# Hybrid decoder layer: key rotations and the first conv blob in the written-order stage, compression later, eight gate columns beside w_out

## Chip, cores and metric

One core of a Trainium2 chip runs the whole layer in one launch. The metric is the device time in microseconds, the median of three runs. TensorE multiplies (PE, with PEld for its weight loads), VectorE is DVE, ScalarE is ACT, GpSimd is POOL, and SP issues most DMAs.

## The reference, cut to what matters

```python
mod_all = silu(c) @ W_ada + b_ada            # 6 x 2048: sh1, sc1, g1, sh2, sc2, g2
h = rms_norm(x, g1n) * (1 + sc1) + sh1       # 512 tokens x 2048
u = h @ w_in                                 # u_b, u_c, u_h, q, kc, vc, ksl, vsl, kwn, vwn, gates
y_conv = u_b * (conv_b + sum_k conv_w[k] * shift(u_c * u_h, 2 - k))
k_cmp = compress(rope(kc)); v_cmp = compress(vc)     # gelu(blocks @ w1) @ w2
y_attn = nsa_attention(rope(q), k_cmp, v_cmp, rope(ksl), vsl, rope(kwn), vwn, sigmoid(gates))
x = x + g1 * (concat(rms_norm(y_conv), rms_norm(y_attn)) @ w_out)
h = rms_norm(x, g2n) * (1 + sc2) + sh2
x = x + g2 * (relu(h @ w_ff1) ** 2 @ w_ff2)
out = rms_norm(x)
```

All arrays are float32. There are 8 query heads and 2 key-value heads of 128, and the feed-forward width is 8192.

## The kernel before

Activations lie transposed: features on the 128 partitions, 512 tokens along the row. Every float32 product is done in three float32r matmuls (`mm3`, L92): high by high, high by low, low by high. So each weight blob of 128 x 1024 (512 KB) that arrives in `raw` is split by `weights` (L76): ACT copies it to `wh` (L83), VectorE subtracts to get `wl` (L84). `raw` has three buffers, `wh` and `wl` two each. A blob is 24 matmuls of 512 columns.

The modulation `mod` is a matrix-vector product that runs on VectorE, not on TensorE: each of its 96 columns is two blobs of `w_ada`, each multiplied with `cs` (the broadcast SiLU of `c`) and summed in one instruction (`dot`, L131), and then a bias (`bias_in`, L137). 32 columns (shift and scale 1) are needed for the first tokens `hs`. The other 64 stand in `todo` (L248): gate 1, scale and shift 2, gate 2. The last is used only in the feed-forward part.

Instructions are ordered by a list scheduler that works before the run, from its own estimates. Where `pinned` is true, `pin` (L67) keeps the written order on each engine instead. Nearly everything up to L361 is pinned: this is the written-order stage. It runs the 32 `steps` of L284 (16 blobs of `w_kv`, 16 of `w_cv`, in four groups), each with eight output tiles in the eight PSUM banks. At a group's end the eight banks are copied into `part` (first half of the depth) or added to it (L346, second half). Group 0 is `w_kv` (keys and values), group 1 the first eight tiles of the conv projection. Step 23 ends group 0, step 31 ends group 1. `clock` and `ready` are the written plan: `ready` grows by 5.6 a step, and the generator `work` (L265) hands out VectorE work with its estimated costs until `clock` comes within 1.0 of `ready`. That work is the columns of `mod` and the tokens; its blobs come into `ring`, eight `wa` buffers (`ada_steps`, L152).

After the stage (unpinned, L363 on), the keys are rotated: `rope` (L367) is four VectorE instructions, `rope_split` (L374) adds an ACT copy and a VectorE subtraction. `kc` takes two `rope`, `kslc` and `kwin` four `rope_split`. Then the loop over `j` (L485) makes the conv output `y` from three tiles each; the tiles after the eighth come from `project` (L400), two halves of one `w_conv` blob each, 32 halves in all. After each half, `tick` advances the first generator in `background` (the two `compress`, L417) and `more_ada(1)` does one further column of `todo`. A compression first adds position vectors (`ct`), splits them (`chi`, `clo`), then takes eight blobs of `cmp_w1` (`swh`, `swl`). The value and gate projections and the queries follow, each with `more_ada(1)` per blob, then attention with the conv half of `w_out`.

The pool `mainp` has 29 slots of 128 x 1032 float32 that nearly all of these tiles share, `cs`, `wa`, `h_m`, `part`, `y` among them; a tile holds its slot until its last reader.

The other half of `w_out` begins at L783: eight loops over `k`, each with one blob from `raw_blob` (L753, six `rw` buffers), split by `hilo` (L762) into one of three `hl` tiles, and 24 matmuls. Eight `w_oa2` blobs are then split and kept, and the feed-forward part follows.

Of the kernel before, what the change touches and what calls it, by code (L numbers as in the profile page):

```python
# [15 lines left out]
P = 128  # L16
# [24 lines left out]
def hybrid_layer(ctx: ExitStack, tc: tile.TileContext, a, out):  # L41
# [84 lines left out]
    pin(nc.vector.tensor_tensor(out=sc, in0=sc, in1=vec[:, V_C:V_ID], op=OP.mult))  # L126
    pin(nc.scalar.activation(small.tile([P, 1], F32, name="junk"), eps, AF.Sqrt))
    ring = [slot(name="wa")[:, :1024] for _ in range(NWA)]
    turn = [0]
# [10 lines left out]

    def ada(n, early=False):
        acc = small.tile([P, 2], F32, name="acc")
        for i in range(2):
            if early:
                w = slot(name="wa")[:, :1024]
                nc.sync.dma_start(out=w, in_=a["w_ada"][2 * n + i])
            else:
                w = load(a["w_ada"][2 * n + i])[:, :1024]
            dot(w, i, acc)
        bias_in(n, acc)  # L150

    def ada_steps(n):  # L152

        acc = small.tile([P, 2], F32, name="acc")
        for i in range(2):
            w = ring[turn[0] % NWA]
            turn[0] += 1
            pin(nc.sync.dma_start(out=w, in_=a["w_ada"][2 * n + i]))
            dot(w, i, acc)
            if i:  # L160
                bias_in(n, acc)
            yield 1.25
# [78 lines left out]
    for i in range(4):  # L241
# [6 lines left out]
    todo = [M_G1 * NK + k for k in range(NK)] + [w * NK + k for k in range(NK) for w in (M_SC2, M_SH2)] \  # L248
        + [M_G2 * NK + k for k in range(NK)]
    done = [0]  # L250
    rb = accum("rb")
# [9 lines left out]
    def low(h, t):  # L261
        pin(nc.vector.tensor_tensor(out=h[:, 1], in0=t, in1=h[:, 0].bitcast(F32), op=OP.subtract))
        hs.append(h)

    def work():  # L265
# [18 lines left out]
    steps = [("w_kv", k) for k in range(4)] + [("w_cv", k) for k in range(8)] \  # L284
        + [("w_kv", k) for k in range(4, NK)] + [("w_cv", k) for k in range(8, NK)]

    def blob(s):
        return weights(a[steps[s][0]][steps[s][1]])
# [25 lines left out]
    banks = {}  # L314
    for s, (name, k) in enumerate(steps):
        grp = 0 if name == "w_kv" else 1
# [21 lines left out]
        if last:  # L338
            for n in range(8):
# [5 lines left out]
                else:  # L345
                    pin(nc.vector.tensor_tensor(out=part[grp, n], in0=ps[n], in1=part[grp, n], op=OP.add))  # L346
                    clock += 0.7
        while clock < ready - 1.0:
            cost = next(flow, None)
            if cost is None:  # L350
                break
            clock += cost
# [4 lines left out]
        if s == 18:  # L357
            pin(nc.scalar.activation(mask_r, cst[:, :C_CMASK - C_MASK], AF.Copy))
    while turn[0] % 2:
        next(flow)  # L360
    pinned[0] = False  # L361

    def more_ada(n, early=True):  # L363
        for _ in range(min(n, len(todo))):
            ada(todo.pop(0), early)

    def rope(dst, ps):  # L367
        t = pair(name="rt")
        nc.vector.tensor_tensor(out=t[:, 0], in0=ps, in1=cos, op=OP.mult)
        nc.vector.tensor_tensor(out=t[0:64, 1], in0=ps[64:128], in1=sin[64:128], op=OP.mult)  # L370
        nc.vector.tensor_tensor(out=t[64:128, 1], in0=ps[0:64], in1=sin[0:64], op=OP.mult)
        nc.vector.tensor_tensor(out=dst, in0=t[:, 0], in1=t[:, 1], op=OP.add)

    def rope_split(dst, ps, scale):  # L374
        t = temp(name="rs2")
        rope(t, ps)
        nc.scalar.activation(dst[:, 0], t, AF.Copy, scale=scale)
        nc.vector.scalar_tensor_tensor(out=dst[:, 1], in0=t, scalar=scale, in1=dst[:, 0].bitcast(F32),
                                       op0=OP.mult, op1=OP.subtract)

    kc = pair(name="kc")
    vc = [part[0, 2], part[0, 3]]
    for g in range(NG):
        rope(kc[:, g], part[0, g])
    kwin = [pair(F32R, name="kwin") for _ in range(NG)]
    kslc = [attc.tile([P, 2, 32 + T], F32R, name=f"kslc{g}") for g in range(NG)]
    for g in range(NG):
        rope_split(kslc[g][:, :, 32:], part[0, 4 + g], 1.0)
        rope_split(kwin[g], part[0, 6 + g], 1.0)

    background = []

    def tick():
# [23 lines left out]
    def compress(which, src):  # L417
# [3 lines left out]
        for hf in range(2):  # L421
# [14 lines left out]
            nc.vector.tensor_tensor(out=lo, in0=t, in1=hi.bitcast(F32), op=OP.subtract)  # L436
            parts.append((hi, lo))
        pc = bank()
        for blk in range(8):
# [39 lines left out]

    background += [compress(0, [kc[:, 0], kc[:, 1]]), compress(1, vc)]  # L480

# [66 lines left out]
    def head(n):  # L548
        q = pair(F32R, name="q")
        rope_split(q, raws[n], SCALE)  # L550
        qs.append(q)
# [645 lines left out]
```

## Time and profile before

| | |
|---|---|
| median of 3 runs | 2250.53 us (2250.18 to 2252.56) |
| profiled execution | 2251.69 us, span 2249.9 us, mean granted clock 0.974 |
| TensorE busy | 2138.4 us, 95% of the span |
| VectorE busy | 1919.1 us, 85% |
| ACT busy | 1009.5 us, 45% |
| HBM traffic | 383.00 MB read, 68.16 MB written |
| dots of `w_ada` | 192 of 1220 ns: 96 from `ring`, 96 after the stage |
| dots in the last eight steps (183.9 to 229.6 us) | 24 |

A matmul's row gives its start and its modelled length; matmuls overlap, so the distance from start to start is the pace. "[11.58 <-DVE wl L84]" means that the engine had been idle for 11.58 us and that VectorE's `wl` at line 84 ended it. Engine shares are means over the whole span; a change in one stage is read from the busy time of that stage and the waits in it.

### The profile page before, as it was taken

How to read it: one execution, taken by the hardware profiler on the slowest of the kernel's cores; microseconds unless marked ns; L12 is line 12 of the kernel's file. 1: busy time of each engine (PE TensorE's matmuls, PEld its weight loads, DVE VectorE, ACT ScalarE, POOL GpSimd, SP SyncE). 2: the span in 40 equal slices, each digit the busy share in tenths (PEclk: the TensorE clock that was granted, in tenths of full speed). 3: DMA queues.
4: the chain of work that ended last, by engine and by line, in shares of the span. 5: the costliest groups of instructions: out<-in, count | busy, mean ns of one | idle time of the engine just before them, and what ended most of it. 6: DMA issues, size and time to landing. Idle time of an engine off the chain costs nothing.

```text
span 2249.9 us, 37644 instructions
## 1 busy us (share of the span) xinstructions
PE 2138.4 (95%) x14942; PEld 1976.7 (88%) x14942; DVE 1919.1 (85%) x2998; ACT 1009.5 (45%) x1468; POOL 193.5 (9%) x366
## 2 busy tenths in 40 slices
PE   6999699999999999899999999999899999999996
PEld 4777478788877769799999999999899999999996
DVE  8889988776586755999999999999899999999995
ACT  4431233222354433766665666656433333333353
POOL 0000000000000000021111111113211011001100
PEclk8999799999999999899999999999999999999998
DMA  8988378756211134176666666668865466366432
GB/s 345 337 319 312 135 287 349 286 210 247 91 50 57 57 113 167 68 223 200 201 206 202 201 195 197 196 207 256 325 244 186 161 234 235 124 224 243 168 114 94
DMA packets 143984, 453.62 MB, mean 202 GB/s; under 512 B 15808, under 2 KB 20160, under 8 KB 143808
## 3 DMA queue, kind: packets, MB, share of 16 engines
q1 hardware_dynamic: 92192, 323.27, 40.2%
q0 software_dynamic: 51616, 127.95, 17.1%
q8 instruction: 117, 1.92, 0.3%
q14 instruction: 59, 0.48, 0.1%
HBM read 383.00 MB, written 68.16 MB: 201 GB/s over the span
## 4 chain that ended last, share of the span: by engine, by line
PE 78%; DVE 13%; ACT 4%; DMA 3%; issue 2%; SPq 0%; DVEq 0%; ACTq 0%
PE pf L93 19%; PE pf L95 19%; PE pf L94 19%; PE ps L95 5%; PE ps L94 5%; PE ps L93 5%; DVE scr L133 3%; DVE wl L84 2%; DMA wa<-in_w_ada 1%; PE pw L94 1%; PE pw L95 1%; PE pw L93 1%; DVE hl L764 1%; PE pt L683 1%; ACT wh L83 1%
## 5 line engine op out<-in xcount | busy, mean ns | idle before, releaser
L95 PE MATMUL pf<-tk,hl 128*128 128x256 f32 x3576 | 1007.1, 282 | 13.0 <-DVE hl L764 13.0
L93 PE MATMUL pf<-tk,hl 128*128 128x256 f32 x3576 | 1009.7, 283 | 9.6 <-ACT hl L763 8.2
L94 PE MATMUL pf<-tk,hl 128*128 128x256 f32 x3576 | 1007.1, 282 | 1.2 <-DVE tk L834 1.2
L95 PEld LDWEIGHTS pf<-tk,hl 128*128 128x128 f32 x3576 | 677.9, 190 | 15.6 <-DVE hl L764 15.5
L93 PEld LDWEIGHTS pf<-tk,hl 128*128 128x128 f32 x3576 | 679.2, 190 | 12.2 <-ACT hl L763 10.9
L94 PEld LDWEIGHTS pf<-tk,hl 128*128 128x128 f32 x3576 | 678.1, 190 | 1.6 <-DVE tk L834 1.5
L763 ACT ACTIVATE hl<-rw 128x1024 fp32r<-128x1024 f32 x266 | 280.8, 1057 | 291.6 <-PE pf L95 266.8
L764 DVE TENSOR_TENSOR hl<-rw,hl 128x1024 fp32r<-128x1024 f32 x266 | 324.5, 1221 | 48.4 <-ACT hl L763 48.0
L763 ACT ACTIVATE hl<-sg 128x1024 fp32r<-128x1024 f32 x189 | 200.4, 1061 | 268.6 <-PE pf L95 241.7
L764 DVE TENSOR_TENSOR hl<-sg,hl 128x1024 fp32r<-128x1024 f32 x189 | 230.8, 1222 | 42.2 <-ACT hl L763 42.1
L133 DVE SCALAR_TENSOR_TENSOR scr<-wa,cs 128x1024 bf16<-128x1024 f32 x192 | 229.7, 1220 | 6.2 <-DMA wa<-in_w_ada 6.1
L83 ACT ACTIVATE wh<-raw 128x1024 fp32r<-128x1024 f32 (+1 forms) x103 | 108.8, 1060 | 238.9 <-PE ps L94 137.9
L84 DVE TENSOR_TENSOR wl<-raw,wh 128x1024 fp32r<-128x1024 f32 (+1 forms) x103 | 126.2, 1227 | 54.9 <-ACT wh L83 54.1
L837 DVE TENSOR_TENSOR sg<-sg,rw 128x1024 f32<-128x1024 f32 x126 | 153.6, 1219 | 0.9
L95 PE MATMUL ps<-h_m,wl 128*128 128x512 f32 x360 | 143.0, 397 | 4.9 <-DVE wl L84 4.8
L93 PE MATMUL ps<-h_m,wh 128*128 128x512 f32 x360 | 142.6, 396 | 1.5 <-DVE part L346 1.0
L94 PE MATMUL ps<-h_m,wh 128*128 128x512 f32 x360 | 141.7, 394 | 0.0
L1011 DVE SCALAR_TENSOR_TENSOR x<-pf,mod,x 128x256 f32<-128x256 f32 x256 | 120.2, 480 | 15.6 <-PE pf L95 12.6
L95 PE MATMUL ps<-h,wl 128*128 128x512 f32 x280 | 114.4, 409 | 17.4 <-DVE wl L84 17.3
L93 PE MATMUL ps<-h,wh 128*128 128x512 f32 x280 | 113.3, 405 | 6.0 <-ACT wh L83 3.2
L94 PE MATMUL ps<-h,wh 128*128 128x512 f32 x280 | 113.1, 404 | 0.0
L977 POOL DMA_DIRECT2D g<-gt x192 | 100.9, 532 | 86.6 <-DVE gt L834 81.6
(306 smaller groups left out, 2971.9 us busy)
## 6 DMA issues: line engine op xcount, KB each, us to landing
rw<-in_w_f SPq DMA_DIRECT2D x262, 512.0 KB, 4.3
wa<-in_w_ada SPq DMA_DIRECT2D x192, 512.0 KB, 6.4
tk<-g POOLq DMA_DIRECT2D x114, 512.0 KB, 8.4
g<-gt POOLq DMA_DIRECT2D x192, 256.0 KB, 5.1
raw<-in_w_conv SPq DMA_DIRECT2D x32, 512.0 KB, 7.2
g<-gb POOLq DMA_DIRECT2D x36, 256.0 KB, 2.3
raw<-in_w_kv SPq DMA_DIRECT2D x16, 512.0 KB, 5.3
raw<-in_w_cv SPq DMA_DIRECT2D x16, 512.0 KB, 5.6
```

The costliest lines, as they stand in the source:

```text
L83: pin(nc.scalar.activation(wh[:, :cols], raw[:, :cols], AF.Copy))
L84: pin(nc.vector.tensor_tensor(out=wl[:, :cols], in0=raw[:, :cols], in1=wh[:, :cols].bitcast(F32), op=OP.subtract))
L93: pin(nc.tensor.matmul(ps, lh, rh, start=start, stop=False, skip_group_check=more))
L94: pin(nc.tensor.matmul(ps, lh, rl, start=False, stop=False, skip_group_check=more))
L95: pin(nc.tensor.matmul(ps, ll, rh, start=False, stop=stop, skip_group_check=more))
L133: pin(nc.vector.scalar_tensor_tensor(out=scr, in0=w, scalar=1.0, in1=cs[i].rearrange("p a b -> p (a b)"), op0=OP.mult, op1=OP.mult, accum_ ...
L683: nc.tensor.transpose(pt[:, r * P:(r + 1) * P], probs[b, r][:, kb * P:(kb + 1) * P], ident)
L763: nc.scalar.activation(dst[0], src, AF.Copy)
L764: nc.vector.tensor_tensor(out=dst[1], in0=src, in1=dst[0].bitcast(F32), op=OP.subtract)
L837: nc.vector.tensor_tensor(out=dst, in0=x, in1=y, op=op)
L977: nc.gpsimd.dma_start(out=gd[p // 4][idx[j]][p % 4 // 2][:, p % 2], in_=g[:, j])
L1011: nc.vector.scalar_tensor_tensor(out=xm, in0=src, scalar=gate, in1=xm, op0=OP.mult, op1=OP.add)
```

## The change

The key rotations become a generator `keys` with costs, pinned. When group 0 is complete (step 23), it takes the place of the column work, which goes on when it is exhausted; from then on `ring` is used with four buffers instead of eight. The first `w_conv` blob is appended as a 33rd step, so that it is loaded and split (pinned) before the last group's additions; `project` takes it from `ahead`. `background` begins with a generator of three empty steps, and `compress` has a further `yield` after its additions. `todo` loses the last eight columns of gate 2; these are done in the `w_out` loop, one per `k`, with blobs from the `rw` buffers.

```diff
-    def ada(n, early=False):
+    def ada(n, blob=None):
         acc = small.tile([P, 2], F32, name="acc")
         for i in range(2):
-            if early:
+            if blob is None:
                 w = slot(name="wa")[:, :1024]
                 nc.sync.dma_start(out=w, in_=a["w_ada"][2 * n + i])
             else:
-                w = load(a["w_ada"][2 * n + i])[:, :1024]
+                w = blob(a["w_ada"][2 * n + i])
             dot(w, i, acc)
         bias_in(n, acc)
...
-            w = ring[turn[0] % NWA]
+            w = ring[turn[0] % (4 if 0 in part_done else NWA)]
...
-        + [M_G2 * NK + k for k in range(NK)]
-    done = [0]
+        + [M_G2 * NK + k for k in range(8)]
...
+    def rope(dst, ps):
+        t = pair(name="rt")
+        pin(nc.vector.tensor_tensor(out=t[:, 0], in0=ps, in1=cos, op=OP.mult))
+        yield 0.65
...
+    def rope_split(dst, ps, scale):
+        t = temp(name="rs2")
+        yield from rope(t, ps)
+        pin(nc.scalar.activation(dst[:, 0], t, AF.Copy, scale=scale))
+        yield 0.0
+        pin(nc.vector.scalar_tensor_tensor(out=dst[:, 1], in0=t, scalar=scale, in1=dst[:, 0].bitcast(F32),
+                                           op0=OP.mult, op1=OP.subtract))
+        yield 0.65
...
+    def keys():
+
+        kk = pair(name="kc")
+        kc.extend(kk[:, g] for g in range(NG))
+        for g in range(NG):
+            yield from rope(kc[g], part[0, g])
+        for g in range(NG):
+            kwin.append(pair(F32R, name="kwin"))
+            pairs = [rope_split(kslc[g][:, :, 32:], part[0, 4 + g], 1.0),
+                     rope_split(kwin[g], part[0, 6 + g], 1.0)]
+            for a_, b_ in zip(*pairs):
+                yield a_ + b_
...
+    steps.append(("w_conv", 0))
...
-    for s, (name, k) in enumerate(steps):
+    for s, (name, k) in enumerate(steps[:-1]):
...
+            if k == NK - 1:
+                part_done.add(grp)
+                if grp == 0:
+                    rest, flow = flow, keys()
         while clock < ready - 1.0:
             cost = next(flow, None)
             if cost is None:
-                break
+                flow = rest
+                continue
             clock += cost
...
+    for cost in flow if flow is not rest else ():
+        pass
     while turn[0] % 2:
-        next(flow)
+        next(rest)
     pinned[0] = False
...
+    ahead = [w]
...
-            wh, wl = weights(src(half))
+            wh, wl = ahead.pop() if ahead else weights(src(half))
...
             parts.append((hi, lo))
+            yield
...
-    background += [compress(0, [kc[:, 0], kc[:, 1]]), compress(1, vc)]
+    background += [iter(range(3)), compress(0, kc), compress(1, vc)]
...
             mm3(pm[i], wh[:, s], wl[:, s], mixa[k][:, 0], mixa[k][:, 1], k == 0, k == 7)
+        ada(M_G2 * NK + 8 + k, raw_blob)
```

More of the change, by code (lines that the diff above doesn't have):

```diff
@@ L127, in hybrid_layer @@
     pin(nc.scalar.activation(small.tile([P, 1], F32, name="junk"), eps, AF.Sqrt))
+    part_done = set()
     ring = [slot(name="wa")[:, :1024] for _ in range(NWA)]
@@ L263, in low @@
         hs.append(h)
+    def rope(dst, ps):
+        t = pair(name="rt")
+        pin(nc.vector.tensor_tensor(out=t[:, 0], in0=ps, in1=cos, op=OP.mult))
+        yield 0.65
+        pin(nc.vector.tensor_tensor(out=t[0:64, 1], in0=ps[64:128], in1=sin[64:128], op=OP.mult))
+        yield 0.65
+        pin(nc.vector.tensor_tensor(out=t[64:128, 1], in0=ps[0:64], in1=sin[0:64], op=OP.mult))
+        yield 0.65
+        pin(nc.vector.tensor_tensor(out=dst, in0=t[:, 0], in1=t[:, 1], op=OP.add))
+        yield 0.65
+    def rope_split(dst, ps, scale):
[5 more added lines that the diff above has]
+                                           op0=OP.mult, op1=OP.subtract))
+        yield 0.65
+    kc, kwin = [], []
+    kslc = [attc.tile([P, 2, 32 + T], F32R, name=f"kslc{g}") for g in range(NG)]
+    def keys():
[9 more added lines that the diff above has]
+                yield a_ + b_
     def work():
@@ L358, in hybrid_layer, with more_ada @@
             pin(nc.scalar.activation(mask_r, cst[:, :C_CMASK - C_MASK], AF.Copy))
+    for cost in flow if flow is not rest else ():
+        pass
     while turn[0] % 2:
-        next(flow)
+        next(rest)
     pinned[0] = False
-    def more_ada(n, early=True):
+    def more_ada(n):
         for _ in range(min(n, len(todo))):
[L365 to L381, printed above, removed]
-    vc = [part[0, 2], part[0, 3]]
[L383 to L389, printed above, removed]
+            ada(todo.pop(0))
+    vc = [part[0, 2], part[0, 3]]
     background = []
+    ahead = [w]
     def tick():
@@ L549, in head @@
         q = pair(F32R, name="q")
-        rope_split(q, raws[n], SCALE)
+        for _ in rope_split(q, raws[n], SCALE):
+            pass
         qs.append(q)
```

## The prediction

> **What bounds the kernel now.** I read the page first: TensorE is busy nearly throughout, except where VectorE is at its densest. In the slices below (56.2 us each) the fifth slice, 225 to 281 us, stands out.
>
> ```profile
> span 2249.9 us, 37644 instructions
> PE   6999699999999999899999999999899999999996
> DVE  8889988776586755999999999999899999999995
> ```
>
> From the rows of busy time by stretch I then cut the stages that the diff touches: the last eight steps of the written-order stage, the 36 us after it, the remaining projections with the compression, and the first `w_out` loop.
>
> ```profile
> 183.00:226.00 43.00, 40.77 (x176) 32.66 (x175) 42.60 (x74) 7.43 (x7) 0.00 (x0) 1.00 0.79 296
> 226.00:262.00 36.00, 14.31 (x51) 10.86 (x51) 33.64 (x52) 10.84 (x14) 0.00 (x0) 0.69 0.23 81
> 262.00:461.00 199.00, 195.08 (x927) 159.59 (x926) 163.69 (x275) 62.47 (x74) 0.00 (x0) 0.99 0.79 301
> 823.00:864.00 41.00, 40.96 (x168) 32.49 (x168) 16.31 (x14) 12.84 (x13) 0.00 (x0) 0.95 0.52 183
> ```
>
> The columns are stretch, length, busy time of PE, PEld, DVE, ACT and POOL, granted clock, DMA share and GB/s. Between 226 and 262 us TensorE works 14.31 of 36 us at a mean clock of 0.69, and VectorE 33.64 of 36. On either side TensorE is nearly full. So this hole is VectorE's. The timeline of TensorE shows what it waited for:
>
> ```profile
> 178.82 0.47 PE L93 MATMUL ps<-h_m,wh 128*128 128x512 f32 x1 [1.01 <-DVE part L346]
> ...
> 220.82 0.50 PE L95 MATMUL ps<-h_m,wl 128*128 128x512 f32 x1 [2.23 <-DVE wl L84]
> ...
> 226.28 0.40 PE L94 MATMUL ps<-h,wh 128*128 128x512 f32 x1
> 238.25 0.80 PE L95 MATMUL ps<-h,wl 128*128 128x512 f32 x1 [11.58 <-DVE wl L84]
> 238.84 0.63 PE L93 MATMUL ps<-h,wh 128*128 128x512 f32 x1
> ...
> 243.11 0.49 PE L94 MATMUL ps<-h,wh 128*128 128x512 f32 x1
> 243.44 0.39 PE L95 MATMUL ps<-h,wl 128*128 128x512 f32 x1
> 243.66 0.39 PE L93 MATMUL ps<-h,wh 128*128 128x512 f32 x1
> 243.90 0.39 PE L94 MATMUL ps<-h,wh 128*128 128x512 f32 x1
> ...
> 251.10 0.40 PE L95 MATMUL ps<-h_m,wl 128*128 128x512 f32 x1
> 261.60 0.48 PE L93 MATMUL ps<-swh,chi 128*66 128x256 f32 x1 [10.11 <-ACT swh L83]
> 261.88 0.63 PE L93 MATMUL ps<-h,wh 128*128 128x512 f32 x1
> ...
> 267.21 0.29 PE L93 MATMUL ps<-swh,chi 128*66 128x256 f32 x1
> 267.34 0.28 PE L94 MATMUL ps<-swl,chi 128*66 128x256 f32 x1
> ```
>
> Three stalls matter: 2.23 us for the low half of the last planned blob, 11.58 us for the low half of the first conv blob, 10.11 us for the first compression blob. VectorE's timeline says why:
>
> ```profile
> 219.54 1.23 DVE L84 TENSOR_TENSOR wl<-raw,wh 128x1024 fp32r<-128x1024 f32 x1
> ...
> 224.85 4.87 DVE L346 TENSOR_TENSOR part<-ps,part 128x512 f32<-128x512 f32 x8
> ...
> 236.98 1.22 DVE L84 TENSOR_TENSOR wl<-raw,wh 128x1024 fp32r<-128x1024 f32 x1
> ...
> 257.86 0.98 DVE L427 TENSOR_TENSOR ct<-kc,cw 128x496 f32<-128x496 f32 x1
> ```
>
> The 1.01 us at 178.82 are a wait for the first of eight additions to free a bank, which the change leaves alone. The `wl` that TensorE wants at 226.7 starts at 236.98, behind eight additions into `part` and the key rotations. The `wl` of 219.54 is late because rotations had already slipped in between the planned work. The compression's last `ct` addition starts only at 257.86.
>
> **Part by part: the rotations.** Their VectorE instructions are these groups:
>
> ```profile
> L369 DVE TENSOR_TENSOR rt<-part,rot x6: 685/692/696, 186.2 to 240.8; 128x512 f32<-128x512 f32 x6
> L370 DVE TENSOR_TENSOR rt<-part,rot x6: 685/686/687, 190.5 to 242.2; 64x512 f32<-64x512 f32 x6
> L371 DVE TENSOR_TENSOR rt<-part,rot x6: 684/685/687, 193.7 to 242.9; 64x512 f32<-64x512 f32 x6
> L372 DVE TENSOR_TENSOR rs<-rt x4: 684/686/687, 233.6 to 244.2; 128x512 f32<-128x512 f32 x4
> L378 DVE SCALAR_TENSOR_TENSOR kwin<-rs,kwin x2: 686/686/686, 238.1 to 245.9; 128x512 fp32r<-128x512 f32 x2
> L133 DVE SCALAR_TENSOR_TENSOR scr<-wa,cs x24: 1217/1222/1229, 183.9 to 229.6; 128x1024 bf16<-128x1024 f32 x24
> L133 DVE DVE_READ_ACCUMULATOR scr<-wa,cs x24: 83/84/93, 185.0 to 230.8; 128x1 f32 x24
> L138 DVE SCALAR_TENSOR_TENSOR mod<-acc,vec x96: 98/219/224, 20.5 to 553.2; 128x1 f32<-128x1 f32 x96
> L505 DVE SCALAR_TENSOR_TENSOR vz<-vz,vec 128x511 f32<-128x511 f32 (+1 forms) x4 | 3.0, 749 | 0.9 <-ACT vz L503 0.9
> L507 DVE TENSOR_TENSOR y<-part,vz 128x512 f32<-128x512 f32 x2 | 1.4, 692 | 0.0
> L436 DVE TENSOR_TENSOR clo<-ct,chi 128x1032 fp32r<-128x1032 f32 x2 | 2.5, 1232 | 1.1 <-ACT chi L435 1.1
> ```
>
> With the two `kc` additions and the two `kslc` lows there are 28, near 0.69 us each, 19 us in all. Eight (the two `kc` heads) already ran before 224.85, unplanned; twenty ran after 230. The change puts all 28 into the plan after step 23, at 0.65 us each: 18.2 us. A step is 24 matmuls of 0.235 (243.66 to 243.90), 5.6 us. Between step 24 and step 30 the plan lets VectorE have about 7 x 4.4 = 31 us beside the blobs (5.6 us a step less 1.2 for its `wl`), so about 12.6 us stay for dots at 1.25: 10 dots in place of most of the 24 of the last row. That is 14 dots, seven columns, less here; the eight columns that go to `w_out` offset them, so the projections' load of dots stays the same within one column. And the eight rotations that overran the plan by 8 x 0.65 = 5.2 us now count in it, so the `wl` of 219.54 should run some 5 us earlier and the 2.23 us go.
>
> **The first conv blob.** It becomes step 32, so its `wl` stands ahead of the eight additions, and TensorE can run on at the end of step 31 as soon as the first addition frees a bank. With it go 11.58 us and the slow clock behind them: from 238.25 to 243.11 stand 11 matmuls (one of 0.59, ten of 0.427) where 243.66 to 243.90 shows 0.24 each: 4.86 - 11 x 0.235 = 2.3 us.
> The Trainium skill (TensorE: Matmul & The Clock Gate, Part 1) says that the clock halves after an idle window of about 3.4 us and takes about 3.4 us of work to return; by its 3.4 us the loss behind a stall would be 1.7, not 2.3, and the sum below 1.5 us smaller for the two stalls. The rows above show about 5 us of slow matmuls behind each, so I keep them.
> What is late next is the second conv blob: its `wl` now queues behind the additions, perhaps one dot (1.22), and the conv gate work of `y` 0 and 1 (each a product, two `vz` sums of 0.75 and a `y` of 0.69: about 6 us). TensorE has 5.6 us of the first half to cover it. No trace shows this order; the bounds are 0 and the whole queue (5 us), and I take 1, since the list of the scheduler usually puts a `wl` between.
>
> **The compression.** A generator of three empty ticks goes first, its end takes a fourth, and a new `yield` separates the additions from the first blob. Before, additions and blob 0 belong to half 1; after, additions to half 5 and blob 0 to half 6, so blob 0's matmuls stand behind 6 x 5.6 = 33.6 us of projection. Gone are 10.11 us and the slow clock: from 261.60 to 267.21 ran 4 matmuls of 512 columns and 18 of 256, at full clock 4 x 0.235 + 18 x 0.118 = 3.1 of 5.6 us, so 2.5 us. What VectorE owes by then, counted from the end of the additions: six `wl` (7.3), `y` 0, 1, 2 with their sums of squares (about 10), six columns of dots at 2.5 (15), two `ct` of 0.98 and a `clo` (3.2), `swl` (1.2): 37 us against 32. So it may be 5 us late if everything goes in program order, 0 if dots are put off; I take 2. The price if it is late as before is 12.6. Both compressions still end in half 26 of 32, so nothing is pushed past the projections.
>
> **The ring of four.** After step 23 only four of eight `wa` buffers are used.
>
> ```profile
> wa<-in_w_ada SPq DMA_DIRECT2D x192, 512.0 KB, 6.4
> rw<-in_w_oa SPq DMA_DIRECT2D x16, 512.0 KB, 4.4
> L763 ACT ACTIVATE hl<-rw 128x1024 fp32r<-128x1024 f32 x266 | 280.8, 1057 | 291.6 <-PE pf L95 266.8 <-DVE rw L837 15.6 <-DVE x L1011 5.3
> ```
>
> Four dots take 4.9 us and a `wl` 1.2, against 6.4 us to landing: each round of four may wait a little; queued behind a waiting dot on VectorE are the next blob's `wl` and, at the end, the additions. With ten dots, two or three rounds: bounds -1 (fewer bytes in flight land sooner) and 4; taken 0.5. The rotations' four ACT copies stand between the `wh` copies on ACT, which is busy 7.43 of 43 us there; taken as nothing.
>
> **Eight columns in `w_out`.** 16 dots of 1.22, their readouts (0.08) and eight biases (0.2): 22 us on VectorE, beside 8 loops of 5.6 us of matmuls. VectorE is busy 16.31 of 41 us there, so 24.7 us are free: nearly full, but hidden. The blobs share the six `rw` buffers, three to a loop, so weights are fetched two loops ahead, not six. SP's queue holds the later weights behind the dots' buffers. Two loops are 11.2 us; a weight blob needs 4.4 to 6.4 to land, 1.06 on ACT and 1.22 (as a `wl`) on VectorE. Behind that come the eight `w_oa2` blobs, started later by about as much. Bounds 0 and 6; taken 1. `cs` stays in two of 29 slots through the attention, where I count at most 27 other tiles alive: 0, at worst 2 us of later `mix`.
>
> **Sum.** Recovered: 2.23 + 11.58 + 2.3 + 10.11 + 2.5 = 28.7 us. Given back: 1 + 2 + 0.5 + 1 = 4.5. Net 24.2 us. The profiled execution took 2251.69 us (span 2249.9 and 1.8 around it), so 2227.5 by its own time; the median of 2250.53 lies 1.2 below it, so 2226.3, rounded **2226**.
>
> **Rivals.** (1) The hole moves instead of closing: VectorE is still owed 37 us in 32, and the order of instructions is fixed beforehand, so a matmul of blob 0 put too early holds all behind it, as at 261.60. Then 12.6 us come back instead of 2: 2236.6. For it: VectorE at 33.64 of 36 us. Against it: twenty rotations (13.8 us) are gone from that stretch and blob 0 has four more halves. (2) The second conv blob's `wl` falls behind all of `y` 0 and 1: 5 us and 2 of slow clock in place of 1: 2232. It is the case in which moving one blob only moves the stall by a half; for it, the order at 236.98, where `wl` stood behind rotations of lesser urgency. (3) Slower: the six `rw` buffers are too few. If the dots of one loop are run only after the next loop's weights, the fetch is one loop ahead, and each loop lasts 6.4 + 1.06 + 1.22 + 2.6 = 11.3 us instead of 5.6: eight times 5.7 is 45 us, giving 2271. It makes the kernel slower from 24.2 / 8 = 3 us a loop. Against it: 24.7 us of free VectorE and 183 GB/s in that stretch. (4) No effect, 2250: the additions and the wait for a bank hold TensorE as long as the `wl` did, and blob 0 stalls as now; 1 us at the start of step 24 is all that the trace shows of that.
>
> **How the numbers follow.** The forecast, 2219 to 2230, has 0.66; rival 1 0.14, rival 2 0.09, rival 3 and its like 0.08, no effect 0.03. A run of this kernel tells no change from one of 0.2% (4.5 us): 0.88 faster, 0.03 the same, 0.09 slower by more. Downwards the range ends where all 28.7 us and the 4 us that TensorE lacks between 262 and 461 (199 - 195.08) go, 2218; upwards it takes in rival 1 with the ring's bound of 4 us: 2240. Left out are rivals 3 and 4 and some of the forecast's own edges.
>
> **What would show it.** Step by step: all 28 rotations between the two groups of eight additions, none after; no TensorE stall over 1 us at step 31; after the second group of additions a stall under 2 us and a granted clock near 1.0 until the compression; its first matmul behind six halves; four `wa` buffers without DMA waits over 1 us; in `w_out` no idle TensorE beside the opening one. The projections should end about 24 us earlier. A TensorE stall of 5 us or more ahead of the first `chi` matmul, or a loop of `w_out` over 6.5 us, would prove the sum wrong.

## Result, and the profile after

| | before | after |
|---|---|---|
| median of 4 runs | 2251.33 us (2250.18 to 2252.56) | 2232.36 us (2229.29 to 2232.97) |
| ratio, 95% interval | | 0.991 (0.9894 to 0.9926) |
| profiled execution, span | 2251.69 us, 2249.9 us | 2229.29 us, 2227.5 us |
| first `w_out` matmul | 822.66 us | 801.71 us |

The kernel is faster by 19.0 us by the medians, 0.9%. The profiled execution of the changed kernel is the shortest of its four; against the profiled execution of before it is 22.4 us shorter. Below, lengths inside the kernel come from that pair.

First the page: span, and busy tenths of TensorE and VectorE in 40 slices of 55.7 us.

```profile
span 2227.5 us, 37650 instructions
PE   6999899999999989799999999999899999999996
DVE  8889988777586677999999999999899999999996
```

The fifth slice, which had a 6 of TensorE, has an 8. (The 8 and the 7 at slices 15 and 17 hold the opening wait of `w_out`, 6.55 us, and waits after its norm, up to 3.7 us; the kernel before has such waits too, 5.07 and up to 3.1 us, some 20 us later in the span.) The rows of busy time by stretch say where the rest of that went (columns as before: stretch, length, PE, PEld, DVE, ACT, POOL, granted clock, DMA share, GB/s):

```profile
183.00:226.00 43.00, 41.78 (x180) 33.52 (x179) 40.40 (x62) 10.09 (x12) 0.00 (x0) 1.00 0.61 216
226.00:262.00 36.00, 35.54 (x154) 28.57 (x153) 32.77 (x53) 11.36 (x14) 0.00 (x0) 1.00 0.65 244
262.00:300.00 38.00, 30.29 (x140) 24.61 (x139) 34.24 (x54) 14.38 (x15) 0.00 (x0) 0.87 0.74 273
300.00:441.00 141.00, 140.55 (x684) 116.11 (x683) 115.94 (x197) 46.07 (x57) 0.00 (x0) 1.00 0.83 311
802.00:843.00 41.00, 40.96 (x165) 32.54 (x165) 30.93 (x50) 8.48 (x8) 0.00 (x0) 0.93 0.95 355
```

The 36 us after the stage are full now: 35.54 us of TensorE at clock 1.00, where there were 14.31 at 0.69. But the next 38 us have a hole of their own, 30.29 us at 0.87. The timeline of TensorE gives the stalls that make up both:

```profile
225.53 0.47 PE L93 MATMUL ps<-h,wh 128*128 128x512 f32 x1 [1.22 <-DVE part L384]
...
232.24 0.50 PE L93 MATMUL ps<-h,wh 128*128 128x512 f32 x1 [0.46 <-ACT wh L83]
...
270.58 0.28 PE L93 MATMUL ps<-swh,chi 128*66 128x256 f32 x1
...
274.64 0.34 PE L94 MATMUL ps<-swl,chi 128*66 128x256 f32 x1 [1.67 <-DVE swl L84]
...
280.37 0.48 PE L93 MATMUL ps<-swh,chi 128*66 128x256 f32 x1 [4.22 <-ACT swh L83]
282.67 0.80 PE L95 MATMUL ps<-h,wl 128*128 128x512 f32 x1 [1.82 <-DVE wl L84]
...
288.79 0.40 PE L94 MATMUL ps<-h,wh 128*128 128x512 f32 x1
...
443.46 1.05 PE L171 MATMUL ps<-ones,sacc 128*128 128x1 f32 x8 [2.91 <-DVE sacc L539]
```

At the boundary 1.22 and 0.46 us are left of 11.58. The compression's first matmul (270.58) comes without a stall, but its second and third blob and the conv blob behind them do not: 1.67, 4.22 and 1.82 us, and a slow clock from 282.67 to 288.79. What VectorE did meanwhile:

```profile
269.94 1.22 DVE L84 TENSOR_TENSOR swl<-raw,swh 128x1024 fp32r<-128x1024 f32 x1
...
274.63 1.22 DVE L134 SCALAR_TENSOR_TENSOR scr<-wa,cs 128x1024 bf16<-128x1024 f32 x1
...
277.65 1.22 DVE L134 SCALAR_TENSOR_TENSOR scr<-wa,cs 128x1024 bf16<-128x1024 f32 x1
...
280.73 0.74 DVE L530 SCALAR_TENSOR_TENSOR vz<-vz,vec 128x510 f32<-128x510 f32 x1
281.39 1.22 DVE L84 TENSOR_TENSOR wl<-raw,wh 128x1024 fp32r<-128x1024 f32 x1
```

From 274.63 to 280.73 two whole columns (four dots) and the first conv gate work stand nearly in a row, and the split `wl` that TensorE wants follows them at 281.39; ACT had copied its high half at 268.21 already. The 4.22 us have a longer chain. The load of that `cmp_w` blob goes out at 273.62, lands at about 279.2, and only then can ACT copy it. The load shows no wait of its own. It stood in SP's queue behind six `w_ada` loads, which went out from 263.64 on as slots came free. First what SP's `w_ada` loads waited for between 262 and 285 us (us in all, times, longest; a fourth wait, for `clo`, was 0.9 us), then the rows of SP and ACT:

```profile
SPq L147 <- DVE scr L134: 2.8, 1, 2.8
SPq L147 <- DVE swl L84: 2.2, 1, 2.2
SPq L147 <- PE ps L95: 1.7, 1, 1.7
```

```profile
263.64 9.93 SPq L147 DMA_DIRECT2D wa<-in_w_ada  x6
273.62 0.42 SPq L73 DMA_DIRECT2D raw<-in_cmp_w  x1
...
279.26 1.06 ACT L83 ACTIVATE swh<-raw 128x1024 fp32r<-128x1024 f32 x1 [0.81 <-DMA raw<-in_cmp_w]
```

Three of the four waits were for VectorE. So both VectorE and the order of the loads are in this chain, and the experiments have to tell what each is worth.

### The profile page after: what moved, and what is told of

It reads as the page before. It is cut to its first block, busy times and chain, and to the rows that moved or that the text cites. A ratio compares the mean times of both kernels' runs of the same rounds, so it can differ in the third digit from the quotient of the medians.

```text
span 2227.5 us, 37650 instructions
## 1 busy us (share of the span) xinstructions
PE 2134.3 (96%) x14942; PEld 1974.1 (89%) x14942; DVE 1918.9 (86%) x2998; ACT 1009.3 (45%) x1468; POOL 193.6 (9%) x366
## 4 chain that ended last, share of the span: by engine, by line
PE 77%; DVE 6%; ACT 2%; issue 1%; DMA 1%; POOL 0%; DVEq 0%; ACTq 0%; POOLq 0%
PE pf L95 19%; PE pf L93 19%; PE pf L94 19%; PE ps L95 4%; PE ps L94 4%; PE ps L93 4%; PE pw L95 1%; PE pw L93 1%; PE pw L94 1%; DVE hl L790 1%; PE pt L709 1%; PE pv L93 1%; PE pv L94 1%; ACT hl L789 0%; PE pv L95 0%
## 5 line engine op out<-in xcount | busy, mean ns | idle before, releaser
L93 PEld LDWEIGHTS pf<-tk,hl 128*128 128x128 f32 x3576 | 678.6, 190 | 12.5 <-ACT hl L789 11.8
L134 DVE SCALAR_TENSOR_TENSOR scr<-wa,cs 128x1024 bf16<-128x1024 f32 x176 | 210.1, 1218 | 3.3 <-DMA wa<-in_w_ada 3.2
```

What stands on the lines that cost most here:

```text
L93: pin(nc.tensor.matmul(ps, lh, rh, start=start, stop=False, skip_group_check=more))
L134: pin(nc.vector.scalar_tensor_tensor(out=scr, in0=w, scalar=1.0, in1=cs[i].rearrange("p a b -> p (a b)"), op0=OP.mult, op1=OP.mult, accum_ ...
```

## Experiments

Three theories for the 8 us that came back at the compression. **VectorE's debt:** the dots of one column a half, put among the compression's splits, are more than VectorE can do. **Queue:** SP's queue is in order, and the blobs' loads wait there behind `w_ada` loads that wait for slots. **Start:** the compression simply starts too early or at the wrong place. Beside that, each part of the change was undone. All times are medians; the difference is to the kernel before on the same chip in the same batch. The last column is the first `w_out` matmul of the profiled execution.

| kernel | time, us | difference | ratio to before, 95% | first `w_out` matmul |
|---|---|---|---|---|
| after | 2232.36 | -19.0 | 0.9894 to 0.9926 | 801.71 |
| pool_queue | 2232.5 | -19.1 | 0.9902 to 0.9931 | 801.88 |
| thin_dots | 2226.17 | -25.6 | 0.9871 to 0.9901 | 794.01 |
| late_columns | 2220.77 | -30.8 | 0.985 to 0.9879 | 788.86 |
| late_four | 2222.72 | -30.7 | 0.9851 to 0.9884 | 789.90 |
| early_compress | 2237.59 | -14.0 | 0.992 to 0.9953 | 809.21 |
| late_early | 2233.08 | -18.7 | 0.9903 to 0.9932 | 800.94 |
| later_compress | 2234.62 | -17.9 | 0.9902 to 0.9932 | 804.93 |
| columns_back | 2235.03 | -16.6 | 0.9914 to 0.9944 | 801.13 |
| late_cols_back | 2242.85 | -9.6 | 0.9932 to 0.9965 | 813.52 |
| keys_only | 2236.07 | -16.4 | 0.9907 to 0.9937 | 806.45 |
| keys_back | 2247.36 | -4.4 | 0.9972 to 0.9992 | 810.18 |
| blob_back | 2233.96 | -17.8 | 0.9909 to 0.9939 | 803.44 |

### What stalls the compression

**late_columns**: no column in the first eight halves.

```diff
+    halves_done = [0]
...
-            more_ada(1)
+            halves_done[0] += 1
+            if halves_done[0] > 8:
+                more_ada(1)
```

> The changed kernel with no modulation columns in the first eight projection halves; the eight columns run later, beside the query projection. Queue theory: what stalls TensorE by 1.67 + 4.22 + 1.82 us near 275 to 283 us, and at half clock for some 6 us after it (2.8 us), is SP's queue, where loads of w_ada wait for a slot that a compression blob or an unfinished dot holds, with the next cmp_w1 and w_conv loads behind them; with no columns there the stall goes, about 10 us less than the changed kernel: 2222. VectorE theory: the dots ahead of the wl and swl on VectorE are the cause, and the same run takes them away: also 2222. Third theory, the blobs of the compression arrive late by themselves (raw has three buffers for two streams): stall of 4 us or more stays, 2230 to 2232.

Measured: 30.8 us under before, and its interval lies wholly below that of the changed kernel. Between 230.77 and 430.64 us TensorE has no stall over 0.4 us. The same stretch, 226 to 281.4 us, in the kernel before, in the changed kernel and in this one:

```profile
226.00:281.40 55.40, 33.72 (x147) 27.21 (x146) 49.86 (x77) 16.69 (x20) 0.00 (x0) 0.75 0.39 138
```

```profile
226.00:281.40 55.40, 48.50 (x218) 38.85 (x217) 52.09 (x85) 19.75 (x22) 0.00 (x0) 0.97 0.66 246
```

```profile
226.00:281.40 55.40, 54.95 (x255) 45.02 (x254) 41.63 (x55) 22.22 (x25) 0.00 (x0) 1.00 0.46 155
```

VectorE was at 49.86 of 55.4 us before, at 52.09 after, at 41.63 here. The change filled TensorE's hole without lightening VectorE: the rotations left, and dots took their room. Both the queue and the VectorE theory had forecast this; the third, that the blobs arrive late by themselves (2230 to 2232), falls. This edit takes loads away too, so it alone doesn't tell the debt from the queue.

**pool_queue**: the column loads behind the stage (not those in `w_out`) go out from GpSimd's queue.

```diff
-                nc.sync.dma_start(out=w, in_=a["w_ada"][2 * n + i])
+                nc.gpsimd.dma_start(out=w, in_=a["w_ada"][2 * n + i])
```

> The changed kernel with the w_ada loads after the written-order stage issued from GpSimd's queue instead of SP's; all else is written as before. Queue theory: the loads of w_conv and cmp_w1 no longer stand behind waiting w_ada loads, the 4.22 and 1.82 us stalls near 280 us go, the 1.67 us for swl stays: 2224 to 2226. VectorE theory: the dots stay where they are, so the stall stays within 1 or 2 us: 2231. If loads from GpSimd's queue take longer to land, dots wait and VectorE holds wl up: above 2235.

Measured: no gain, where the queue theory had 2224 to 2226. SP has no `w_ada` loads to hold its blobs up now, and a stall is there, one split further on, ended by VectorE:

```profile
286.52 0.48 PE L94 MATMUL ps<-swl,chi 128*66 128x256 f32 x1 [5.13 <-DVE swl L84]
```

ACT had copied its high half by 280.8; ahead of that `swl` (285.25) VectorE did conv gate work and two dots, at 280.59 and 282.71. So the queue was on the path of the 4.22 us, but taking the loads off it saves nothing: VectorE is late there without it too. As the cause of the lost time the queue theory falls.

**thin_dots**: the dots of the first eight halves take 128 of 1024 columns, so this kernel leaves out seven eighths of eight modulation columns; loads, buffers and order of issue stay.

```diff
+        n = 128 if thin[0] > 0 else 1024
-        pin(nc.vector.scalar_tensor_tensor(out=scr, in0=w, ...
+        pin(nc.vector.scalar_tensor_tensor(out=scr[:, :n], in0=w[:, :n], ...
...
             more_ada(1)
+            thin[0] -= 1
```

> The changed kernel in which the 16 dots of the first eight halves multiply 128 of their 1024 columns (so seven eighths of eight modulation columns are left out); their 512 KB loads, buffers and order of issue stay. It takes about 16 x 1.07 = 17 us from VectorE there. Theory (VectorE time is what holds the compression's first blobs): no stall over 1.5 us at the compression, 2221 to 2224. Rival (the loads or the shared buffers hold them): stalls of 7 us together stay, 2230 to 2233.

Measured: 2226.2 us, between the two forecasts, with an interval that overlaps that of the changed kernel by its edge. A dot now takes 0.29 us instead of 1.22. The trace says more: of 1.67, 4.22 and 1.82 us one wait of 1.69 us is left between 240 and 350 us, and it is for ACT's copy.

```profile
275.80 0.50 PE L93 MATMUL ps<-h,wh 128*128 128x512 f32 x1 [1.69 <-ACT wh L83]
```

So most of the stall goes with VectorE's time alone, the loads unchanged: the first `w_out` matmul comes 7.7 us earlier than in the changed kernel. It is still 5.2 us later than in late_columns, which has neither dots nor loads there. Whether that rest (the 1.69 us, a wait of 1.54 us at 358.27) goes with the loads or with what is left of the dots is not shown.

**late_four**: as late_columns, with `halves_done[0] > 4`.

> The kernel in which the columns wait, but four halves instead of eight, so that two columns (four dots, 5 us) still stand ahead of the compression's first blob. Theory (it is VectorE's debt ahead of the first compression blob that stalls TensorE; four halves without dots leave room enough, and four columns fewer slide into the attention's start): no stall over 1.5 us at the compression, 2219 to 2223. Rival (the dots that stand among the compression's own splits hold them): stalls of 3 us or more together there, 2225 to 2230.

Measured: the same as eight within the intervals, 30.7 us under before; no stall over 0.4 us stands between 232.33 and 432.22 us. Its row of the stretch, and the splits and dots that VectorE started in it (groups: count, durations, first and last start), then those of the changed kernel:

```profile
226.00:281.40 55.40, 54.94 (x255) 45.01 (x254) 51.78 (x77) 21.67 (x25) 0.00 (x0) 1.00 0.64 228
```

```profile
L84 DVE TENSOR_TENSOR wl<-raw,wh x10: 1217/1225/1229, 231.4 to 280.4; 128x1024 fp32r<-128x1024 f32 x10
L84 DVE TENSOR_TENSOR swl<-raw,swh x4: 1215/1218/1223, 257.6 to 275.1; 128x1024 fp32r<-128x1024 f32 x4
L134 DVE SCALAR_TENSOR_TENSOR scr<-wa,cs x11: 1214/1222/1226, 229.6 to 278.0; 128x1024 bf16<-128x1024 f32 x11
```

```profile
L84 DVE TENSOR_TENSOR wl<-raw,wh x8: 1206/1218/1226, 231.4 to 281.4; 128x1024 fp32r<-128x1024 f32 x8
L84 DVE TENSOR_TENSOR swl<-raw,swh x2: 1219/1219/1219, 269.9 to 273.4; 128x1024 fp32r<-128x1024 f32 x2
L134 DVE SCALAR_TENSOR_TENSOR scr<-wa,cs x17: 1178/1218/1226, 229.5 to 278.8; 128x1024 bf16<-128x1024 f32 x17
```

VectorE is as busy as in the changed kernel, 51.78 of 55.4 us against 52.09. But six dots fewer have made room for four splits more, 14 instead of 10, and it is for the splits that TensorE waits. So dots among the compression's splits are harmless when the halves before them were free of dots, and the second theory of this run falls. (Like late_columns, the run takes away the loads of those halves too; that VectorE's time counts without them is thin_dots' part.)

### When the compression starts

**early_compress**: the changed kernel without the delay.

```diff
-    background += [iter(range(3)), compress(0, kc), compress(1, vc)]
+    background += [compress(0, kc), compress(1, vc)]
...
             parts.append((hi, lo))
-            yield
```

> The changed kernel with the compression at its old place: no three empty steps, no extra yield, so its additions and first blob belong to the first projection half. If delaying the compression is worth what the prediction's sum says, the 10 us stall in front of the first chi matmul returns, less the 14 us of rotations that VectorE no longer has there: the first blob then waits for y 0 and 1, ct, chi and swl, 4 to 10 us and 2.5 us of half clock: 2233 to 2240. If the delay only moved the stall (rival 1), the time is that of the changed kernel, 2232.

**late_early**: both edits, columns late and no delay.

> The columns wait eight halves, and the compression starts at once as in the kernel before (no empty steps, no separate step between additions and first blob). Theory (what the delay buys is time for VectorE to work off the dots): with no dots in the way the compression needs little delay, stall under 3 us before its first matmul, 2221 to 2224. Rival (the additions and split of the compression themselves need the delay, as the 8.08 us stall of the kernel without delay suggests): a stall of 5 us or more stays, 2226 or above.

Measured: 14.0 and 18.7 us under before. early_compress is within its forecast of 2233 to 2240; for late_early the rival held (a stall of 5 us or more, 2226 or above). The first matmul with `chi` of each:

```profile
247.44 0.48 PE L93 MATMUL ps<-swh,chi 128*66 128x256 f32 x1 [8.08 <-ACT swh L83]
```

```profile
244.32 0.48 PE L93 MATMUL ps<-swh,chi 128*66 128x256 f32 x1 [8.08 <-ACT swh L83]
```

The stall is 8.08 us with the dots and without: here it is the additions, copies and splits of the compression itself, for which TensorE waits. The first theory of late_early, that the delay only buys time for dots, falls. But an early start alone does not make this stall. keys_only (below) starts at once too, without the 33rd step and the columns in `w_out`; its last addition into `part` starts at 224.79, here at 230.25, and its first `chi` matmul (242.06) waits 0.35 us.

By differences to before, the delay alone brings 5.0 us (14.0 to 19.0), the waiting of the columns alone 4.7 (14.0 to 18.7), and both together 16.8. The intervals of the single edits overlap that of early_compress; by the first `w_out` matmul they bring 7.5, 8.3 and 20.4 us. By either measure the two are worth more together than added.

**later_compress**: `iter(range(8))` instead of `iter(range(3))`.

> The changed kernel with eight empty steps ahead of the compression instead of three, so that its first blob comes eleven halves after the stage, not six. Theory (VectorE owes more per half than it can do while columns run at one a half: 2.5 of dots, 1.2 of a split and the conv gate work of about 2 in 5.6 us is just about what fits, so waiting lets it work off the debt slowly): stalls of 1 to 4 us remain, 2226 to 2230. Rival (any start collides with the dots of the same halves): stalls of 7 us, 2231 to 2234. Second rival (five halves are ample): no stall over 1 us, 2221.

Measured: 17.9 us under before, not told apart from the change. None of its `chi` matmuls waits over 0.4 us. But TensorE waits for VectorE's half of a conv blob instead (3.14 us), at the end of the first compression (2.31 us), and at the end of the second (3.78 us), which now lies past the projections, where nothing covers its waits:

```profile
275.65 0.50 PE L95 MATMUL ps<-h,wl 128*128 128x512 f32 x1 [3.14 <-DVE wl L84]
...
357.24 0.33 PE L484 MATMUL ps<-vec,hid 64*128 64x64 f32 x2 [2.31 <-DVE hid L481]
...
442.83 1.61 PE L502 MATMUL ps<-cw,hpad 128*128 128x128 f32 x8 [3.78 <-DVE hpad L498]
```

None of the three theories names that end; the time lies just above the second's (2231 to 2234), the mechanism is another. So a later start brings nothing that the intervals can tell, and an earlier one costs 7.5 us by the first `w_out` matmul: the place of the compression alone is not what is missing.

### The columns in `w_out`

**columns_back**: all 16 columns of gate 2 in `todo`, none in the `w_out` loop.

```diff
-        + [M_G2 * NK + k for k in range(8)]
+        + [M_G2 * NK + k for k in range(NK)]
...
-        ada(M_G2 * NK + 8 + k, raw_blob)
```

> The changed kernel with the eight gate columns back in todo and none in the w_out loop (they then run beside the query projection, which has VectorE free). If the w_out columns cost what the trace shows (the idle time before the first w_out matmul is 6.55 us against 5.07), 1.5 us come back there: 2230.5. If they cost nothing: 2232. If the rest of todo had needed the room, VectorE holds up the queries or the first out_conv: 2235 or more.

**late_cols_back**: the same edit in late_columns.

> The kernel in which the columns wait eight halves, with all 16 columns of gate 2 among them and none in w_out. Theory (in the projections after the compression VectorE has room for them): the same as with eight in w_out, 2220 to 2222, the first w_out matmul 2 us later at most. Rival (the eight columns in w_out are what makes the waiting affordable): stalls of 3 us or more at the end of the projections or in the attention's start, 2224 or above.

Measured: in the changed kernel the edit costs 2.4 us by the differences (2235.03, the time of the third theory), but the intervals overlap, and the first `w_out` matmul is 0.6 us earlier: not told from nothing. In late_columns it costs 21.2 us, and the rival holds. Columns that had waited are still undone in the attention, where VectorE is needed: 22 dots start after 560 us, against 6 in late_columns. Stretch 570 to 640 us of late_cols_back, and two of its stalls:

```profile
570.00:640.00 70.00, 52.32 (x220) 40.25 (x218) 61.94 (x149) 23.37 (x61) 0.00 (x0) 0.78 0.48 175
```

```profile
602.26 0.80 PE L95 MATMUL pw<-mix,wl 128*128 128x512 f32 x1 [3.67 <-DVE wl L84]
...
616.27 0.79 PE L93 MATMUL pw<-mix,wh 128*128 128x512 f32 x1 [4.61 <-ACT wh L83]
```

With the eight columns in `w_out` the same stretch has 66.15 us of TensorE at 0.98:

```profile
570.00:640.00 70.00, 66.15 (x337) 52.96 (x336) 58.57 (x151) 34.90 (x91) 0.00 (x0) 0.98 0.19 61
```

So this part shows no gain in the change as made, and is what makes the waiting of the columns affordable.

### Rotations and first conv blob

**keys_back**: the rotations after the stage, unordered; `work` goes on instead, ring of eight.

```diff
-            w = ring[turn[0] % (4 if 0 in part_done else NWA)]
+            w = ring[turn[0] % NWA]
...
-                if grp == 0:
-                    rest, flow = flow, keys()
...
     pinned[0] = False
+    for cost in keys():
+        pass
```

> The changed kernel with the rotations left unordered after the stage, as before, the column work never replaced, and the ring at eight buffers; the conv blob, the delay and the w_out columns stay. Theory (the rotations are what crowded VectorE at the boundary): 28 rotations, 19 us, come back into the 36 us after the stage, 14 dots, 17 us, leave the halves that follow; the stall shows as 8 to 12 us in the first halves or ahead of the compression, time about 2241 (2237 to 2246). Rival (dots and rotations are the same VectorE time, so only the first conv blob and the delay count): 2232 to 2234, no stall over 3 us before the first matmul with chi.

**keys_only**: the changed kernel with the edits of blob_back (below), early_compress and columns_back together, so only rotations and ring are left of the change.

> The kernel before with one part of the change: the rotations ordered by hand between step 23 and the last additions, and the ring of four from there. The first conv blob, the compression's start and the gate columns stay as before. Theory (the parts are worth most together; the rotations carry about 15 us of it, as the kernel without them shows): the stall at the last planned step goes, the conv blob's stall shrinks to about 4 us as in the kernel without the 33rd step, the compression's stays at 8 us: 2240 (2236 to 2243). Rival (VectorE's list just puts dots where the rotations stood): 2247 or more.

**blob_back**: no 33rd step.

```diff
-    steps.append(("w_conv", 0))
...
-    for s, (name, k) in enumerate(steps[:-1]):
+    for s, (name, k) in enumerate(steps):
...
-    ahead = [w]
+    ahead = []
```

> The changed kernel without the 33rd step: the first conv blob is loaded and split by the scheduler again, after the stage. Theory (two causes held its low half: the eight additions ahead of it and the rotations that slipped in): with the rotations gone the low half stands behind the additions alone, 4.9 us and 1.2 of its own less the 2 us in which TensorE works with the high half: a stall of 3 to 5 us, time about 2237. Rival (place is all): 11.6 us and 2.3 of slow clock come back, 2246. Second rival (the scheduler puts the low half ahead of the additions by itself): 2232.

Measured: the rotations with the ring of four bring 16.4 us of the 19.0, everything but them 4.4 us, all but the blob 17.8 us. In keys_only the time is at the lower edge of the theory's 2236 to 2243; the conv blob waits 3.06 us, as forecast, but the compression's stall of 8 us does not stay (0.35 us). Without the rotations in the plan (keys_back) the 2.23 us at the last planned step are back, a stall of 3.21 us follows, and the compression stalls by 5.84 although its start is delayed:

```profile
219.99 0.63 PE L95 MATMUL ps<-h_m,wl 128*128 128x512 f32 x1 [2.23 <-DVE wl L84]
...
237.84 0.80 PE L95 MATMUL ps<-h_m,wl 128*128 128x512 f32 x1 [3.21 <-DVE wl L84]
...
284.68 0.48 PE L93 MATMUL ps<-swh,chi 128*66 128x256 f32 x1 [5.84 <-ACT swh L83]
```

Its median is above both forecasts, by more than these stalls. By the first `w_out` matmul it is 12.5 us ahead of before, by the median only 4.4. In the profiled execution, the fastest of its ten, 4.8 us of that gap lie behind this matmul, in code that is the same (last section); the rest is between executions. So what the rotations are worth when taken away lies between 8.5 us (first `w_out` matmul, 810.18 - 801.71) and 14.6 us (medians, 19.0 - 4.4), and that stays open. Without the 33rd step (blob_back) the first blob's low half is late by 4.33 us instead of 11.58, as the first theory had it:

```profile
228.66 0.80 PE L95 MATMUL ps<-h,wl 128*128 128x512 f32 x1 [4.33 <-DVE wl L84]
```

Yet the time is only 1.2 us above the change by the differences (forecast 2237, measured 2233.96, intervals overlapping, so the step's worth is not told from nothing). After a further 2.32 us at a conv blob (244.54) the waits at the compression are only 0.86, 1.56 and 0.70 us. A likely reading is that while TensorE waits earlier, VectorE works off what it owes; no run tests it by itself.

## Why the prediction was right, and where it was off

The forecast was 2226, with 2219 to 2230 as its likely stretch and a range of 2218 to 2240; measured were 2232.36 by the median and 2229.29 in the profiled execution. The direction and most terms held. One term was mis-sized by 8.6 us, so the median lies beyond the likely stretch, in the part of the range that was meant for rival 1.

- **The rotations.** All 28 ran between 184.5 and 207.5 us, and ten dots after them in the stage, as counted. First and last group of them, from the instructions by line:

```profile
L267 DVE TENSOR_TENSOR rt<-part,rot x6: 683/684/686, 184.5 to 201.0; 128x512 f32<-128x512 f32 x6
L281 DVE SCALAR_TENSOR_TENSOR kwin<-rs,kwin x2: 687/688/689, 198.3 to 207.5; 128x512 fp32r<-128x512 f32 x2
```

- **2.23 us at the last planned step, recovered:** gone, as taken; no stall over 0.4 us is left there.
- **11.58 + 2.3 us at the first conv blob, recovered; 1 given back:** 1.22 and 0.46 us remain, 1.7 in all. The second blob's low half was not late, so rival 2 did not happen.
- **Ring of four, 0.5 given back:** TensorE lost nothing by it; two splits waited 0.88 and 0.84 us for ACT on VectorE.
- **10.11 + 2.5 us at the compression, recovered; 2 given back.** This is the term that was mis-sized. The stall at the old place went, but 1.67 + 4.22 + 1.82 = 7.7 us returned, and 14 matmuls from 282.67 to 288.79 took 6.12 us where 0.232 each (3.25 us) is the pace at a granted clock of 1.00: 2.9 us more. Together 10.6 where 2 were taken.
- **Why it was mis-sized.** The sum "37 us against 32" miscounted twice. The new `yield` stands inside the loop over the two sets of additions, so each compression stops there twice: blob 0 belongs to half 7, not 6, and the compressions end with tick 28, not in half 26. In the trace eight halves of 24 matmuls stand ahead of 270.58. And there are four `ct` and two `clo` in it (6.5 us), not two and one (3.2). Measured, VectorE worked 38.36 of the 41.67 us from the end of the last addition into `part` to the end of the first `swl` (229.49 to 271.16). Blob 0 was in time, then, partly because it stood two halves later than the sum had it, and because columns were put off: of the sixteen dots of these eight halves ten had run. The sum stopped there. The six dots owed run from 271.07 to 280.0, among the splits of the next blobs. That is rival 1's mechanism at the blobs behind the one that it named: its price was 12.6 us, of which 10.6 came.
- **What the runs show of the cause.** With the same loads and shorter dots (thin_dots) one wait of 1.69 us is left of the three; without dots in the halves before (late_columns, late_four) none. With the loads off SP's queue (pool_queue) the loss stays.
- **Columns in `w_out`, 1 given back:** the loops lost nothing, with 30.93 us of VectorE in 41. The opening wait grew from 5.07 to 6.55 us, but columns_back has 6.17 and late_columns 5.09, so the columns are not the cause; what is stays open. Rival 3 did not happen: six `rw` buffers were enough at 355 GB/s.
- **Not in the forecast's sum:** three stalls of the kernel before, beyond 282 us, are gone, 3.6 us. The forecast had them only in the range's lower end. keys_only and early_compress, which start the compression at once, keep the last two, so they go with the delay; by what path is not shown.

```profile
282.61 0.50 PE L95 MATMUL ps<-h,wl 128*128 128x512 f32 x1 [1.01 <-DVE wl L84]
...
325.27 0.50 PE L95 MATMUL ps<-h,wl 128*128 128x512 f32 x1 [1.57 <-DVE wl L84]
...
395.10 0.50 PE L95 MATMUL ps<-h,wl 128*128 128x512 f32 x1 [1.04 <-DVE wl L84]
```

Together 28.7 - 1.7 - 10.6 + 3.6 = 20.0 us. The first norm matmul moved from 464.49 to 443.46, 21.0 us, and the first `w_out` matmul by 20.95. The median's 19.0 is smaller still; the part behind that matmul differs by more than this from one execution to the next (last section). Part of the agreement is luck: the 3.6 us that no term held and 1.5 us of prices that did not come (ring and loops) made up for more than half of the 8.6. Without them the time would have been near 2237, rival 1's.

The step that the eight columns in `w_out` offset the seven that left the stage, so that "the projections' load of dots stays the same", was not needed, and not how the code works. `more_ada(1)` does one column a half while `todo` lasts: before, after and keys_only all have 64 dots between the last addition into `part` and the norm behind the halves. What the eight columns change is the number of dots behind the halves and ahead of `w_out`: 30 in the changed kernel, 46 in keys_only, 32 before.

## What to carry to other kernels

Here the stalls that ended with a late engine went when work was taken from that engine in that stretch. Moving the consumer alone left 10.6 us of stall and slow clock at the next blobs that the engine owed, of the 12.6 us taken away. So carry the debt sum on past the first consumer: add up work and time half by half until the engine has caught up, and put off what is due last (here columns of gates, shifts and scales of later stages; letting them wait eight halves brought 11.8 us further). And see where the work that was put off comes to lie: without its eight columns in `w_out` the same line lost more than it won.

## What the runs showed of the hardware

**The clock.** Behind stalls matmuls of 512 columns started 0.43 us apart for a while, instead of 0.23. These slow phases were not of one length. Behind 3.21 us (keys_back, 237.84) seven matmuls ran slow, 3.0 us; behind 11.58 us in the kernel before it was 4.9; behind 1.67, 4.22 and 1.82 us in the changed kernel 6.1. In later_compress the clock fell only after work had resumed: the first matmuls behind the 3.14 us stall (275.65, 275.99) still start 0.3 us apart, the slow ones begin at 276.30 and end at 279.63. A stall of 2.23 us (kernel before, 220.82) left no slow matmuls. The Trainium skill (TensorE: Matmul & The Clock Gate, Part 1) puts both the idle window and the return at about 3.4 us, with a free-running window, so that the slow length varies from run to run. The runs agree with the varying, but stalls of 3.06 us (keys_only, with 1.71 us of idle just before) and 3.21 us were already enough, and the slow phases lasted up to 6.1 us.

**The pace of a full TensorE.** In the feed-forward part the same matmuls at a granted clock of 1.00, with TensorE at 100 of 100 us, came to 846 to 852 in 100 us, depending on the execution. keys_back, 200 us behind its first `w_out` matmul, and the changed kernel at the same place:

```profile
1010.18:1110.18 100.00, 100.00 (x846) 100.00 (x845) 91.01 (x121) 61.16 (x86) 18.41 (x35) 1.00 0.65 201
```

```profile
1001.71:1101.71 100.00, 100.00 (x851) 100.00 (x851) 91.77 (x122) 61.77 (x87) 18.42 (x35) 1.00 0.63 199
```

The rest of the kernel from the first `w_out` matmul on took 1425.8 to 1432.1 us in the 14 profiled executions. What sets the pace isn't in the trace. It means that changes of a few us in one stage are better read from where a later matmul stands than from the end.

**Loads.** During the `w_out` loops the DMA engines moved 355 GB/s at a share of 0.95 without one TensorE stall in the loops.
